# Low parts of 64 weight blocks made on VectorE instead of GpSimd, in a two-layer encoder trunk

## The chip, the cores and the metric

The kernel runs on 1 core of one Trainium2 chip. The metric is device time in microseconds, the median of several executions; one more execution is taken with the hardware profiler. The core's engines are named as the profile names them: PE (TensorE, matmuls; PEld its weight loads), DVE (VectorE), ACT (ScalarE), POOL (GpSimd) and SP (SyncE, which starts the transfers).

## The reference, cut to what matters

One step of a streaming encoder with two layers, for a prompt of 1024 rows and a sample of 64 rows that share all weights. All in float32.

```python
for i in range(2):
    hn = rmsnorm(x, norm_mix_g[i])
    x = x + (pool_mix(hn, ...) if i == 0 else hgrn_mix(hn, ...))
    x = x + conv_ffn(rmsnorm(x, norm_ffn_g[i]), ...)
x = rmsnorm(x, norm_out_g)

def pool_mix(h, ...):             # four windows, 256 columns each
    d = windowed_mean(h) - h      # causal, windows of 2, 4, 8, 16 rows
    return concat([d[g] @ w[g] for g in range(4)]) * scale

def conv_ffn(h, hist, w_up, cw, cb, w_down):
    gate, val = split(h @ w_up)   # 1024 -> 2 x 2816
    conv = cb + sum(cw[j] * shifted(gate, j) for j in range(3))
    return (silu(conv) * val) @ w_down
```

Layer 1's mixer is HGRN2, a gated linear recurrence in chunks of 64 rows.

## The kernel before, in words

**Layout.** The rows (1024 of the prompt, 64 of the sample) lie along the free axis in three chunks, 384, 384 and 256 + 64 columns; the model's 1024 features lie on 128 partitions x 8. `x` stays in SBUF for the whole run.

**Products in three terms.** A float32 product is made of fp32r products. Every weight block of 128 x 512 arrives raw (f32) in one of five buffers of the pool `raw`, by a transfer that SP starts (L134). ACT casts it to its high part `whi` (L128) and POOL subtracts to get the low part `wlo` = raw - whi (L129). With the activations split in the same way (`split`, L185 and L186: `hnhi` and `hnlo`, `hh` and `hl`), `mm3` issues three matmuls for each product: whi by the high part (L180), whi by the low part (L181), wlo by the high part (L182).

**The weight queue.** `load_ready` (line 109) goes through `queue` in order. A block is taken when one of 8 slots (a pair of `whi` and `wlo`) is free, and `drop` frees a slot when PE's last use of it has been issued. The raw buffer is free again for SP's next load when the subtract that reads it is done. The keys are ("pw", g, half) for the pooling mixer's pointwise weights, ("up", layer, block, part) and ("dn", layer, block, half) for the ConvFFN, and others for the HGRN mixer. For some parts `q_mix` loads two raw blocks and adds or subtracts them on DVE first (L152).

**Layer 0's mixer.** `token_sums` and `pool_diffs` scale the window matrices by each row's 1/rms (`rstd`, a Newton chain of small DVE steps, L333 to L344; `wr`, L544) and multiply (`pd`, L565); `pool_mix` multiplies by `pw` into `pe` and DVE updates `x` (L594).

**Norms.** `norm` sums the squares of `x` over the 8 feature blocks (L366, L373 into `acc_f`), PE transposes the sum (`nps_f`, L378), `rstd` gives the factor, and DVE makes the normed rows (L417).

**ConvFFN.** The 22 blocks of 128 hidden features are taken two at a time, 11 groups. Group 0 (blocks 0 and 1) makes plain products with the parts a11, a12, a21 and a22. From group 1 (blocks 2 and 3) on, chunks 0 and 1 are multiplied together as a 2 x 2 block product with seven products, whose mixed activations `sums` makes on DVE (sums at L437 and L449, split at L186) while group 0 and the start of group 1 run, and whose mixed weights come from `q_mix` (nine parts). Products land in banks `px`, `py`, `pz`; DVE adds them up in `e` (L713); ACT copies the gate (`ge`, L684); the convolution is two steps on DVE (L630, L631) between two on ACT; `hidden` multiplies and splits (L640, L642); `down` multiplies by the `dn` weights into `dn` banks, and DVE adds each to `x` (L757), which frees the bank (five banks, pool `pB`).

**Who sets the order.** PE's order is a schedule written by hand: tasks are generators whose yields carry costs, and `run` merges them under `tc.manual_schedule`. DVE, ACT, POOL and SP are ordered by the Tile scheduler, so an instruction that changes its engine shifts its neighbours on both. Each engine issues in order and waits in order.

Of the kernel before, what the change touches and what calls it, by code (L numbers as in the profile page):

```python
# [9 lines left out]
F32 = mybir.dt.float32  # L10
# [4 lines left out]
ALU = mybir.AluOpType  # L15
# [50 lines left out]
def trunk_kernel(ctx: ExitStack, tc: tile.TileContext, xtok, xs_tok, hist_tok, xf, par, gmix, pw, winm, ident_in,  # L66
                 masks_in, w_up, w_dn, w_in, w_out, s0, y_out, npool, nhg, nconv):
    nc = tc.nc
# [37 lines left out]
    free = [(i, False) for i in range(NR)]  # L106
    extra_w = []

    def load_ready(most=None):

        while queue and (most is None or len(loaded) < most):
            ph, key, make = queue[0]
            own = [p for p in free if p[1]] if ph == "g" and key[:2] not in (("out", H - 2), ("out", H - 1)) else []
            p = own[0] if own else next((p for p in free if not p[1]), None)
            if p is None:
                return
            free.remove(p)
            queue.pop(0)
            places[key] = p
            i, extra = p  # L120
            nm = "_".join(str(k) for k in key)
            if extra:
                hi, lo = (extra_w[i // 2][:, (i % 2 * 2 + b) * HW_:(i % 2 * 2 + b + 1) * HW_] for b in range(2))
            else:
                hi = wp.tile([P, HW_], F32R, name=f"whi{nm}", tag=f"whi{i}", bufs=1)
                lo = wp.tile([P, HW_], F32R, name=f"wlo{nm}", tag=f"wlo{i}", bufs=1)
            src = make(nm)
            nc.scalar.copy(hi, src)  # L128
            nc.gpsimd.tensor_tensor(lo, src, hi.bitcast(F32), op=ALU.subtract)  # L129
            loaded[key] = (hi, lo)  # L130

    def raw_block(nm, src, i):
# [24 lines left out]
    def drop(*keys):  # L157

        for k in keys:
            p = places.pop(k)  # L160
            free.append(p)
        load_ready()
# [320 lines left out]
    def token_sums(c):  # L483
# [19 lines left out]
        if c == 0:  # L503
            for i in (1, 0):
                nc.sync.dma_start(wm[i], winm[i])
            nc.sync.dma_start(ident, ident_in)
            load_ready(2)
            nc.sync.dma_start(prm, par)
# [13 lines left out]
        if c == 0:  # L522
            load_ready(6)
# [656 lines left out]
```

## Time and profile before

| | us |
|---|---|
| median of 3 executions (2372.25 to 2373.45) | 2372.37 |
| the profiled execution | 2377.06 |
| its span in the profile | 2375.2 |
| PE busy | 2284.7 (96%) |
| DVE busy | 1613.8 (68%) |
| POOL busy | 1003.0 (42%) |
| ACT busy | 904.3 (38%) |

The mean granted clock of PE is 0.981 of full speed. The span is that of the profiled execution and is 1.9 us shorter than its time; it is cut into stretches below. Busy time of an engine is the time in which it runs instructions of its own, not the time in which it waits. Idle time is put down to the instruction that ended it (the releaser). Where consecutive instructions of one kind are shown in one row, "x2" or "x3" stands at its end and the duration is that of all.

### The profile page before, as it was taken

How to read it: one execution, taken by the hardware profiler on the slowest of the kernel's cores; microseconds unless marked ns; L12 is line 12 of the kernel's file. 1: busy time of each engine (PE TensorE's matmuls, PEld its weight loads, DVE VectorE, ACT ScalarE, POOL GpSimd, SP SyncE). 2: the span in 40 equal slices, each digit the busy share in tenths (PEclk: the TensorE clock that was granted, in tenths of full speed). 3: DMA queues.
4: the chain of work that ended last, by engine and by line, in shares of the span. 5: the costliest groups of instructions: out<-in, count | busy, mean ns of one | idle time of the engine just before them, and what ended most of it. 6: DMA issues, size and time to landing. Idle time of an engine off the chain costs nothing. (4 is left out here: it accounts for less than half of the span.)

```text
span 2375.2 us, 38111 instructions
## 1 busy us (share of the span) xinstructions
PE 2284.7 (96%) x13830; PEld 2231.3 (94%) x13830; DVE 1613.8 (68%) x3728; ACT 904.3 (38%) x1965; POOL 1003.0 (42%) x1054
## 2 busy tenths in 40 slices
PE   9889999999999989999999999889999999999996
PEld 8889999999999989999999999878999999999996
DVE  6786656566666688767667767778766666666567
ACT  5444333334433353323323322345333333443335
POOL 1155554556655562112112211224454555564555
PEclk8999999999999999999999999989999999999998
DMA  7123333333433321001011000102343334433431
GB/s 233 49 81 116 125 121 120 123 125 129 138 116 125 124 69 36 26 18 54 26 35 40 32 26 22 36 25 76 111 130 116 125 119 134 134 124 117 129 120 76
DMA packets 118099, 218.70 MB, mean 92 GB/s; under 512 B 13436, under 2 KB 17404, under 8 KB 117528
## 3 DMA queue, kind: packets, MB, share of 16 engines
q1 hardware_dynamic: 117822, 216.15, 28.0%
q8 instruction: 109, 1.79, 0.3%
q14 instruction: 78, 0.64, 0.1%
q10 hardware_dynamic: 90, 0.12, 0.0%
HBM read 210.51 MB, written 5.72 MB: 91 GB/s over the span
## 5 line engine op out<-in xcount | busy, mean ns | idle before, releaser
L129 POOL TENSOR_TENSOR wloup_a<-rawup_a,whiup_a 128x512 fp32r<-128x512 f32 x368 | 513.1, 1411 | 568.1 <-ACT whiup_a L128 534.4
L128 ACT CAST whiup_a<-rawup_a 128x512 fp32r<-128x512 f32 x368 | 224.2, 617 | 573.8 <-PE dn L181 397.4
L152 DVE TENSOR_TENSOR rawup_a<-rawup_a,rawup_a 128x512 f32<-128x512 f32 x200 | 186.6, 933 | 286.4 <-DMA rawup_a<-w_up_in 261.4
L180 PE MATMUL dn<-hh,whidn 128*128 128x384 f32 (+1 forms) x1056 | 351.5, 333 | 11.5 <-DVE x L757 8.0
L181 PE MATMUL dn<-hl,whidn 128*128 128x384 f32 (+1 forms) x1056 | 348.7, 330 | 0.7 <-DVE hl L186 0.7
L182 PE MATMUL dn<-hh,wlodn 128*128 128x384 f32 (+1 forms) x1056 | 348.9, 330 | 0.0
L757 DVE TENSOR_TENSOR x<-x,dn 128x384 f32<-128x384 f32 (+1 forms) x528 | 262.3, 528 | 97.1 <-PE dn L182 95.5
L180 PEld LDWEIGHTS dn<-hh,whidn 128*128 128x128 f32 x1056 | 200.2, 190 | 18.0 <-DVE x L757 13.4
L181 PEld LDWEIGHTS dn<-hl,whidn 128*128 128x128 f32 x1056 | 200.1, 190 | 1.3 <-DVE hl L186 1.3
L182 PEld LDWEIGHTS dn<-hh,wlodn 128*128 128x128 f32 x1056 | 200.1, 189 | 0.0
L180 PE MATMUL pj<-hnhi,whiin 128*128 128x384 f32 (+1 forms) x528 | 185.0, 350 | 1.1 <-ACT hnhi L185 1.1
L181 PE MATMUL pj<-hnlo,whiin 128*128 128x384 f32 (+1 forms) x528 | 173.0, 328 | 2.4 <-POOL hnlo L186 2.4
L182 PE MATMUL pj<-hnhi,wloin 128*128 128x384 f32 (+1 forms) x528 | 173.2, 328 | 0.0
L630 DVE SCALAR_TENSOR_TENSOR cv<-ge,prm,cv 128x322 f32<-128x322 f32 (+1 forms) x132 | 132.1, 1002 | 48.2 <-ACT cv L629 42.0
L129 POOL TENSOR_TENSOR wlodn<-rawdn,whidn 128x512 fp32r<-128x512 f32 x88 | 119.0, 1354 | 100.9 <-ACT whidn L128 76.8
L960 DVE COPY_PREDICATED at<-masks,pl 128x64 f32<-128x64 uint8 (+7 forms) x432 | 117.0, 293 | 50.5 <-PE pl L945 48.8
L632 ACT ACTIVATE cv<-cv 128x322 f32<-128x322 f32 (+1 forms) x132 | 67.2, 509 | 161.3 <-DVE cv L631 160.9
L180 PE MATMUL pv<-hnhi,whiup_a 128*128 128x320 f32 (+1 forms) x384 | 122.1, 318 | 0.0
L180 PE MATMUL pg<-hnhi,whiup_a 128*128 128x320 f32 (+1 forms) x384 | 122.1, 318 | 0.0
L182 PE MATMUL pg<-hnhi,wloup_a 128*128 128x320 f32 (+1 forms) x384 | 121.7, 317 | 0.0
L182 PE MATMUL pv<-hnhi,wloup_a 128*128 128x320 f32 (+1 forms) x384 | 121.5, 317 | 0.0
L181 PE MATMUL pg<-hnlo,whiup_a 128*128 128x320 f32 (+1 forms) x384 | 121.5, 316 | 0.0
(1234 smaller groups left out, 6199.0 us busy)
## 6 DMA issues: line engine op xcount, KB each, us to landing
rawup_a<-w_up_in SPq DMA_DIRECT2D x568, 256.0 KB, 2.8
rawdn<-w_dn_in SPq DMA_DIRECT2D x88, 256.0 KB, 3.1
rawin<-w_in_in SPq DMA_DIRECT2D x64, 256.0 KB, 2.6
rawupp_a<-w_up_in SPq DMA_DIRECT2D x16, 256.0 KB, 2.7
rawout<-w_out_in SPq DMA_DIRECT2D x16, 256.0 KB, 2.7
xt<-xtok_in SPq DMA_DIRECT2D x7, 448.0 KB, 6.7
x<-xf_in SPq DMA_DIRECT2D x2, 1536.0 KB, 8.7
y_out<-x SPq DMA_DIRECT2D x8, 384.0 KB, 2.3
```

The lines of the kernel that those rows point to most:

```text
L128: nc.scalar.copy(hi, src)
L129: nc.gpsimd.tensor_tensor(lo, src, hi.bitcast(F32), op=ALU.subtract)
L152: nc.vector.tensor_tensor(t[0], t[0], t[1], op=bs[2])
L180: nc.tensor.matmul(ps, w[0][:, wsl], a_hi, start=first, stop=False, skip_group_check=more)
L181: nc.tensor.matmul(ps, w[0][:, wsl], a_lo, start=False, stop=False, skip_group_check=more)
L182: nc.tensor.matmul(ps, w[1][:, wsl], a_hi, start=False, stop=last, skip_group_check=more)
L630: nc.vector.scalar_tensor_tensor(t[:, :wd], ge[:, 0:wd], prm[:, cw[0]:cw[0] + 1], t[:, :wd], op0=ALU.mult, op1=ALU.add)
L632: nc.scalar.activation(t[:, :wd], t[:, :wd], AF.Silu)
L757: nc.vector.tensor_tensor(x[c][:, d, :], x[c][:, d, :], pd[:, :n], op=ALU.add)
L960: nc.vector.copy_predicated(dst[:, :, :, d * hh:], mk, a)
```

## The change

A function chooses the engine for the low part by the block's key: DVE for all of the pooling mixer's pointwise weights, for the up weights of ConvFFN blocks 0 to 3 and the down weights of blocks 0 and 1, in both layers; POOL for the rest. Of the subtracts at L129 (now L132), 64 move: 4 of `pw`, and per layer 26 of `up` (4 plain parts for each of two blocks, 9 parts for each of the next two) and 4 of `dn`. The instruction is otherwise the same. Behind the three added lines every line number of the kernel is 3 higher.

```diff
     extra_w = []
+
+    def lo_engine(ph, key):
+        return nc.vector if key[0] == "pw" or key[0] in ("up", "dn") and key[2] < (4, 2)[key[0] == "dn"] else nc.gpsimd
 
     def load_ready(most=None):
...
             src = make(nm)
             nc.scalar.copy(hi, src)
-            nc.gpsimd.tensor_tensor(lo, src, hi.bitcast(F32), op=ALU.subtract)
+            lo_engine(ph, key).tensor_tensor(lo, src, hi.bitcast(F32), op=ALU.subtract)
             loaded[key] = (hi, lo)
```

What it does to DVE's order is shown at three places. The first is DVE at the start of layer 0's mixer: `nt_p` is the Newton chain, `wr` the scaled window matrices that `pd` reads. Before:

```order
L343 TENSOR_TENSOR nt_p_202<-nt_p_202 128x4
L344 SCALAR_TENSOR_TENSOR nt_p_202<-nt_p_202 128x4
L544 TENSOR_SCALAR wr_214<-wm_105,nt_p_202 96x384
L544 TENSOR_SCALAR wr_218<-wm_104,nt_p_202 112x384
L463 TENSOR_TENSOR lbt<-prm 128x8
```

With the change:

```order
L347 SCALAR_TENSOR_TENSOR nt_p_202<-nt_p_202 128x4
L547 TENSOR_SCALAR wr_214<-wm_105,nt_p_202 96x384
L132 TENSOR_TENSOR wlopw_0_150<-rawpw_0_151,whipw_0_149 128x512
L547 TENSOR_SCALAR wr_218<-wm_104,nt_p_202 112x384
L132 TENSOR_TENSOR wlopw_1_156<-rawpw_1_157,whipw_1_155 128x512
```

Two low parts of the pointwise weights now stand behind the first and behind the second `wr`.

The second place is DVE in the third norm ahead of layer 0's ConvFFN (chunk 2): `acc_f` are the sums of squares, the last row ends them. Before:

```order
L366 TENSOR_TENSOR acc_f_1018<-acc_f_1018,sq_f_1022 128x320
L366 TENSOR_TENSOR acc_f_1019<-acc_f_1019,sq_f_1025 128x320
L152 TENSOR_TENSOR rawup_2_a_0_1405<-rawup_2_a_0_1405,rawup_2_a_3_1407 128x512
L366 TENSOR_TENSOR acc_f_1018<-acc_f_1018,sq_f_1028 128x320
L366 TENSOR_TENSOR acc_f_1019<-acc_f_1019,sq_f_1031 128x320
L630 SCALAR_TENSOR_TENSOR cv_1_0_1068<-ge_1_0_1064,prm,cv_1_0_1068 128x384
L366 TENSOR_TENSOR acc_f_1018<-acc_f_1018,sq_f_1034 128x320
L366 TENSOR_TENSOR acc_f_1019<-acc_f_1019,sq_f_1037 128x320
L631 SCALAR_TENSOR_TENSOR cv_1_0_1068<-ge_1_0_1064,prm,cv_1_0_1068 128x384
L373 TENSOR_TENSOR acc_f_1019<-acc_f_1019,acc_f_1018 128x320
```

With the change:

```order
L132 TENSOR_TENSOR wloup_1_a_995<-rawup_1_a_0_996,whiup_1_a_994 128x512
L132 TENSOR_TENSOR wloup_1_a_1001<-rawup_1_a_1_1002,whiup_1_a_1000 128x512
L132 TENSOR_TENSOR wloup_1_a_1007<-rawup_1_a_2_1008,whiup_1_a_1006 128x512
L132 TENSOR_TENSOR wloup_1_a_1013<-rawup_1_a_3_1014,whiup_1_a_1012 128x512
L369 TENSOR_TENSOR acc_f_1018<-acc_f_1018,sq_f_1022 128x320
L369 TENSOR_TENSOR acc_f_1019<-acc_f_1019,sq_f_1025 128x320
L369 TENSOR_TENSOR acc_f_1018<-acc_f_1018,sq_f_1028 128x320
L369 TENSOR_TENSOR acc_f_1019<-acc_f_1019,sq_f_1031 128x320
L369 TENSOR_TENSOR acc_f_1018<-acc_f_1018,sq_f_1034 128x320
L369 TENSOR_TENSOR acc_f_1019<-acc_f_1019,sq_f_1037 128x320
L155 TENSOR_TENSOR rawup_2_a_0_1405<-rawup_2_a_0_1405,rawup_2_a_3_1407 128x512
L376 TENSOR_TENSOR acc_f_1019<-acc_f_1019,acc_f_1018 128x320
```

Four low parts of block 1's up weights now stand ahead of the sums, and the two convolution steps of group 0 have gone behind them.

The third place is DVE in group 1 of layer 0, ahead of the addition to `e` of block 2 (`sum` and `mix0w` are the mixed activations, `cv` the convolution). Before:

```order
L449 TENSOR_TENSOR sum_1477<-row0w_930,row0q_873 128x384
L449 TENSOR_TENSOR sum_1479<-row0w_930,row0x 128x384
L449 TENSOR_TENSOR sum_1481<-row0w_930,row0q_873 128x384
L630 SCALAR_TENSOR_TENSOR cv_1_2_1505<-ge_1_2_1498,prm,cv_1_2_1505 128x322
L152 TENSOR_TENSOR rawup_2_a_2_1650<-rawup_2_a_2_1650,rawup_2_a_3_1652 128x512
L631 SCALAR_TENSOR_TENSOR cv_1_2_1505<-ge_1_2_1498,prm,cv_1_2_1505 128x322
L186 TENSOR_TENSOR mix0w_1568<-sum_1475,mix0w_1568 128x384
L186 TENSOR_TENSOR mix0w_1568<-sum_1477,mix0w_1568 128x384
L713 TENSOR_TENSOR e_2_1566<-e_2_1566,px_2_1573 128x384
```

With the change:

```order
L452 TENSOR_TENSOR sum_1477<-row0w_930,row0q_873 128x384
L452 TENSOR_TENSOR sum_1479<-row0w_930,row0x 128x384
L452 TENSOR_TENSOR sum_1481<-row0w_930,row0q_873 128x384
L132 TENSOR_TENSOR wloup_2_a_1493<-rawup_2_a_2_1494,whiup_2_a_1492 128x512
L633 SCALAR_TENSOR_TENSOR cv_1_2_1505<-ge_1_2_1498,prm,cv_1_2_1505 128x322
L132 TENSOR_TENSOR wlodn_0_0_1523<-rawdn_0_0_1524,whidn_0_0_1522 128x512
L634 SCALAR_TENSOR_TENSOR cv_1_2_1505<-ge_1_2_1498,prm,cv_1_2_1505 128x322
L132 TENSOR_TENSOR wlodn_1_0_1541<-rawdn_1_0_1542,whidn_1_0_1540 128x512
L189 TENSOR_TENSOR mix0w_1568<-sum_1475,mix0w_1568 128x384
L189 TENSOR_TENSOR mix0w_1568<-sum_1477,mix0w_1568 128x384
L716 TENSOR_TENSOR e_2_1566<-e_2_1566,px_2_1573 128x384
```

One low part of an up weight and two of the down weights have come in ahead of the addition; the raw sum of L152 has left this piece.

## Rows read from the trace of the kernel before

**Rows 1.** The page, part 1: busy time, share of the span and instructions
```profile
PE 2284.7 (96%) x13830; PEld 2231.3 (94%) x13830; DVE 1613.8 (68%) x3728; ACT 904.3 (38%) x1965; POOL 1003.0 (42%) x1054
```

**Rows 2.** Stretches: length, busy per engine, clock, DMA share, GB/s
```profile
120.00:180.00 60.00, 53.61 (x326) 51.87 (x325) 53.92 (x92) 27.75 (x59) 34.45 (x30) 1.00 0.26 84
300.00:360.00 60.00, 60.00 (x368) 60.00 (x367) 35.15 (x59) 22.77 (x44) 34.91 (x39) 1.00 0.39 128
1580.00:1640.00 60.00, 53.52 (x313) 51.03 (x311) 54.27 (x105) 33.60 (x71) 23.29 (x27) 0.97 0.17 54
```

**Rows 3.** Waits of PE, 120 to 180: us in total, times, longest
```profile
PE px L181 <- DVE hnlo L186: 1.9, 1, 1.9
PE py L180 <- ACT ge L684: 1.9, 1, 1.9
PE px L180 <- DVE e L713: 1.6, 1, 1.6
PE dn L180 <- DVE x L757: 0.9, 1, 0.9
```

**Rows 4.** Waits of PE, 1620 to 1680
```profile
PE px L180 <- ACT hnhi L185: 2.8, 2, 2.6
PE px L181 <- DVE hnlo L186: 2.3, 2, 1.9
PE dn L180 <- DVE x L757: 1.6, 2, 1.1
```

**Rows 5.** Waits of PE in 0 to 60, 60 to 120, 1500 to 1560
```profile
PE pd L565 <- DVE wr L544: 3.9, 1, 3.9
...
PE nps_f L378 <- DVE acc_f L373: 6.1, 2, 3.9
...
PE pl L945 <- DVE q__16127 L936: 7.3, 2, 3.9
```

**Rows 6.** Timeline of DVE, 136 to 162: start, us, line, operation
```profile
137.21 1.20 DVE L437 TENSOR_TENSOR sum<-row0w,row0x 128x384 f32<-128x384 f32 x1
...
140.84 1.65 DVE L437 TENSOR_TENSOR sum<-row0w 128x384 f32<-128x384 f32 x1
...
144.44 0.55 DVE L437 TENSOR_TENSOR sum<-row0q,row0w 128x384 f32<-128x384 f32 x1
...
153.00 1.54 DVE L186 TENSOR_TENSOR hl<-hr,hh 128x320 fp32r<-128x320 f32 x1
...
160.67 0.48 DVE L186 TENSOR_TENSOR hl<-hr,hh 128x320 fp32r<-128x320 f32 x1
```

**Rows 7.** POOL: two pieces of its timeline; its group on the page
```profile
12.47 1.26 POOL L129 TENSOR_TENSOR wlopw<-rawpw,whipw 128x512 fp32r<-128x512 f32 x1 [11.54 <-ACT whipw L128]
...
140.45 3.19 POOL L129 TENSOR_TENSOR wloup_a<-rawup_a,whiup_a 128x512 fp32r<-128x512 f32 x2
...
L129 POOL TENSOR_TENSOR wloup_a<-rawup_a,whiup_a 128x512 fp32r<-128x512 f32 x368 | 513.1, 1411 | 568.1 <-ACT whiup_a L128 534.4
```

**Rows 8.** Timeline of DVE, 1619 to 1642, first and last of the hits
```profile
1620.22 2.59 DVE L437 TENSOR_TENSOR sum<-row1w 128x384 f32<-128x384 f32 x3
...
1640.85 1.62 DVE L186 TENSOR_TENSOR hnlo<-sum,hnhi 128x384 fp32r<-128x384 f32 x1
```

**Rows 9.** DVE's sum of two raw blocks: one of the timeline; the group
```profile
156.80 0.68 DVE L152 TENSOR_TENSOR rawup_a<-rawup_a,rawup_a 128x512 f32<-128x512 f32 x1
...
L152 DVE TENSOR_TENSOR rawup_a<-rawup_a,rawup_a 128x512 f32<-128x512 f32 x200 | 186.6, 933 | 286.4 <-DMA rawup_a<-w_up_in 261.4
```

**Rows 10.** Timeline of DVE: Newton steps near 12, 46 and 1527
```profile
12.34 0.16 DVE L338 TENSOR_TENSOR nt_p<-nt_p 128x4 f32<-128x4 f32 x1
12.54 1.22 DVE L339 SCALAR_TENSOR_TENSOR nt_p<-nt_p 128x4 f32<-128x4 f32 x1
...
46.51 1.20 DVE L342 TENSOR_SCALAR nt_f<-nt_f 128x3 f32<-128x3 f32 x1
...
1527.21 1.23 DVE L340 TENSOR_TENSOR nt_g<-nt_g 128x3 f32<-128x3 f32 x1
```

## The prediction

> **What bounds the kernel now.** I read the busy shares first. TensorE (PE) is busy for 96% of the span; VectorE (DVE) for 68%, GpSimd (POOL) for 42% [rows 1]. The table of stretches says where the missing 4% lies: in the middle of a ConvFFN PE has 60.00 of 60 us and DVE 35, so nothing given to DVE there can be seen; in the 60 us in which each ConvFFN opens, PE loses about 6.5 us and DVE is busy for 54 of 60 [rows 2]. So the change is judged by PE's own waits, and by DVE in the openings. The waits of PE in the two openings [rows 3, 4] and in three other stretches [rows 5] name a DVE instruction as the releaser nearly everywhere, and ACT where it runs behind DVE. None names POOL's low part: PE never waits for the thing whose engine is changed.
>
> What it waits for is DVE's list, and that list is slowed. A subtract or sum of DVE of 128x384 takes 0.55 us when alone and 1.65 when a low part of POOL runs beside it: the call at 140.84 lies on POOL's pair of 140.45 [rows 6, 7]. Calls that read one input from PSUM keep their time in the same stretch. From the first to the last I count eight long calls ahead of the e<-px that PE waits for at 158.8 us: 1.20 at 137.21, 1.64, 1.65, 1.65, a pair of 2.86 (1.02 when not hit), 1.65, and 1.54 against 0.48 at 153.00 [rows 6]. Their excess is 0.65 + 1.09 + 1.10 + 1.10 + 1.84 + 1.10 + 1.06 = 7.9 us. In layer 1 the same count from the triple at 1620.22 (2.59 against 1.49) to the 1.62 at 1640.85 gives eight hits and 8.2 us [rows 8]. POOL's subtracts are lengthened too: 1.26 alone, 1.41 in the mean, 3.19 for a pair [rows 7].
>
> **The change part by part.** 64 subtracts go from POOL to DVE: the mixer's 4, and in each layer 26 of up weights and 4 of down weights. PE's order is the same. Nothing is removed, and no DMA is added; a raw buffer is now given back to SP's next weight load by a DVE instruction.
>
> *Price of one on DVE.* No DVE subtract with an fp32r result of this size is in the trace. The nearest row is the sum of two raw blocks, same shape, both inputs in SBUF: 0.68 us unhit, 0.93 in the mean with its hits [rows 9]. I take 0.68, because the subtract that hit it is the one that moves; 0.93 stays as the upper bound. A lower bound is 0.55 x 512/384 = 0.73 less the 0.1 by which neighbours overlap: 0.6.
>
> *Layer 0, first two groups.* Ahead of e<-px the changed DVE order holds eight moved subtracts, and one raw sum (L152) has gone behind it. Gain 7.9 + 0.68 - 8 x 0.68 = 3.2 us earlier, out of the 1.9 + 1.9 + 1.6 that PE waits there [rows 3]. The wait of 0.9 for the x update of the down product goes too, since DVE is then ahead. Term: **4.1**.
>
> *Layer 1, first two groups.* 8.2 - 8 x 0.68 - 0.47 (a sum of L449 that now comes earlier) = 2.3; I take 2.0 of the 5.1 of px, as part of it waits for ACT [rows 4]. The two dn waits of 1.6 go. Term: **3.6**.
>
> *Start.* One Newton step is hit: 1.22 instead of 0.16, with POOL's wlopw running [rows 7, 10]. Without it wr comes 1.06 earlier, the second wr only 0.4, since wlopw now stands between them. The products pd wait for the first [rows 5]. Term: **0.6**. First norm: two steps are hit, the second taking 1.20 [rows 10], which gives back 2.0; two moved calls cost 1.36; of the 0.64 PE sees about **0.5**.
>
> *Third norm of layer 0.* Here the change costs. Four moved subtracts (2.7 us) come ahead of the sums of squares, on whose end (acc_f) PE waits up to 3.9 us [rows 5]; in exchange the two conv steps and the raw sum between them move behind or later, 0.61 + 0.61 + 0.68 back. Term: **-0.8**.
>
> *End of the HGRN mixer.* The steps of the Newton chain at 1524 to 1531 are hit several times (1.23 against 0.16) [rows 10], partly by POOL's sums of squares, which stay. Two hits go (2.0), two moved calls come (1.4): **0.6**, against waits of 7.3 us at pl [rows 5].
>
> Everything else lies in stretches where PE is full, and DVE has 25 us of 60 free: nothing. What would take that cover away is a DVE instruction that waits in order for an ACT cast whose slot PE has not freed; behind it stand the x updates that free the five PSUM banks of dn. A slot is freed ahead of those updates, so I price this at nothing and give it a rival. For SP: the raw buffer that DVE returns comes about 2 us later than from POOL, and the load then still reaches its slot before PE's use of it.
>
> Sum: 4.1 + 3.6 + 0.6 + 0.5 - 0.8 + 0.6 = 8.6. The profiled execution took 2377.1 us (its span 2375.2 and 1.9 around it), 4.7 above the median of the runs: 2368.5 for a like profile, and 2372.4 - 8.6 = **2363.8 us** for the runs. With 0.93 for each of the sixteen priced calls the openings lose 4.0 and the sum is 4.6 (2367.8); with 0.6 they gain 1.3 (2362.5).
>
> A rule that speaks against this: the Trainium skill, Perfetto Trace Analysis, section Identifying the Most-Contended Engine, has the engine of highest occupancy relieved first; of the two at hand that is DVE (68% against 42%), and the change loads it by 44 us. By it the kernel would lose; the trace shows why the share misleads here: DVE is idle where PE is full, and in the openings its time goes to hits.
>
> **The rivals.** (a) *Given back.* The relief comes, but the next waiter on PE is late as well, such as ACT's casts, or a DVE wait in order for a raw block. For it: the py wait names ACT [rows 3], the longest px wait of layer 1 does too [rows 4]. Against: ACT's input there comes from DVE. Then only the start and a third of the openings stay: 2.6 + 0.5, less 0.8, some 2 us: 2370.
>
> (b) *Slower: the hits do not go, DVE only gets longer.* If the long calls come from the order in which DVE and POOL happen to start, or from something else in the openings, the moved calls are pure load: eight at 0.6 in each opening (4.8 + 4.8), four each at the third norm and at the start (2.4 + 1.8, less what PE has free), 0.6 and 1.2 at the HGRN end and the first norm, together 15.6: 2388. It decides from the point where a moved call costs more than the relief per call, 7.9 / 8 = 0.99 us; the row nearest is 0.68. For it: some hits in the HGRN stretch are from POOL work that stays. Against: all sixteen hits of the openings lie on a low part. The Trainium skill, SBUF — State Buffer, section Who interferes with whom, says that a DVE instruction with two SBUF inputs contends with a POOL instruction that reads SBUF, and that the order of issue decides who blocks. The trace agrees on the first: 1.65 against 0.55; by the second POOL alone would be held where DVE starts first, and the rows show both lengthened.
>
> (c) *More.* DVE being ahead removes the whole of the openings' waits (6.3 + 6.7), and the start, the first norm and the HGRN end give their full hits (1.1 + 2.0 + 1.4): 17.5 us, 2355. For it: once DVE keeps up, the queue no longer grows. Against: eight new calls stand in each opening.
>
> **How the numbers follow.** A difference of about 0.2% (4.7 us) is what a measurement of this kernel can tell from no change: faster is below 2367.6, slower above 2377.1. Chances: forecast 0.48 (2360 to 2368), more (c) 0.16, given back (a) 0.21, slower (b) and its milder forms 0.15. Faster 0.64, same 0.21, slower 0.15. The range takes in the forecast, most of (c) and all of (a) but not (b): **2356 to 2376**; the likeliest case alone is 2360 to 2368.
>
> **What would show it.** Right: in the changed profile DVE's sums and subtracts at 137 to 155 and 1620 to 1641 us are at 0.55, the new DVE subtracts at 0.6 to 0.7, PE's waits for px, py and dn in the openings fall from 13 to about 5 us, pd starts near 14.2 instead of 15.24, and the wait for acc_f in the third norm grows. Given back: the same DVE rows, but PE's waits keep their sum under another name. Wrong: DVE rows stay at 1.65, or the new subtracts take 1.0 or more; or a wait appears in the full stretches, at dn or at a weight load, where rows 2 show none.

## The result and the profile after

| | us |
|---|---|
| kernel before, median of 6 (2371.96 to 2375.55) | 2372.85 |
| changed kernel, median of 6 (2352.36 to 2364.69) | 2363.62 |
| ratio | 0.995, 95% interval 0.9933 to 0.9967 |
| profiled execution, before and after | 2377.06 and 2364.69 |
| the changed kernel twice more, each beside the kernel before | 0.9964 (0.9951 to 0.9977) and 0.9928 (0.9911 to 0.9946) |

The forecast was 2363.8 us; the gain is 9.2 us in the medians and 12.4 between the two profiled executions. Three sets of runs put it between 8 and 16 us.

Part 1 of the page of the changed kernel:

```profile
PE 2281.5 (97%) x13830; PEld 2229.7 (94%) x13830; DVE 1609.8 (68%) x3792; ACT 905.4 (38%) x1965; POOL 915.6 (39%) x990
```

DVE has 64 instructions more than in [rows 1], and is busy for 4.0 us less (0.3 and 8.0 less in the two later profiles of the changed kernel). POOL is busy for 87 us less: 64 subtracts of 1.3 to 1.4 us. The price of a moved one is in the view of its source line: instructions on DVE, shortest / median / longest in ns, first and last start.

```profile
L132 DVE TENSOR_TENSOR wloup_a<-rawup_a,whiup_a x52: 676/685/784, 28.6 to 1686.2; 128x512 fp32r<-128x512 f32 x52
...
L132 DVE TENSOR_TENSOR wlodn<-rawdn,whidn x8: 678/683/693, 150.8 to 1640.7; 128x512 fp32r<-128x512 f32 x8
...
L132 DVE TENSOR_TENSOR wlopw<-rawpw,whipw x4: 681/682/682, 13.8 to 28.0; 128x512 fp32r<-128x512 f32 x4
```

The price is 0.68 us, the row of L152 that was taken for it [rows 9]; 64 of them are 43.8 us, and the hits (DVE calls lengthened beside a subtract on POOL) that went gave back at least as much. In DVE's timeline of the changed kernel, the calls of the opening (line numbers 3 higher than in [rows 6]):

```profile
135.37 0.55 DVE L440 TENSOR_TENSOR sum<-row0w,row0x 128x384 f32<-128x384 f32 x1
...
138.31 0.55 DVE L440 TENSOR_TENSOR sum<-row0w,row0f 128x384 f32<-128x384 f32 x1
...
144.55 1.02 DVE L189 TENSOR_TENSOR hnlo<-sum,hnhi 128x384 fp32r<-128x384 f32 x2
...
147.02 0.48 DVE L189 TENSOR_TENSOR hl<-hr,hh 128x320 fp32r<-128x320 f32 x1
...
153.44 0.54 DVE L716 TENSOR_TENSOR e<-e,px 128x384 f32<-128x384 f32 x1
```

The calls that took 1.20, 1.65 and 1.54 us take 0.55, 0.55 and 0.48, and the pair of 2.86 takes 1.02. The addition to `e` starts at 153.44 instead of the 158.81 of the kernel before:

```profile
158.81 0.54 DVE L713 TENSOR_TENSOR e<-e,px 128x384 f32<-128x384 f32 x1
```

Of these 5.4 us, 1.8 were won ahead of 136 us already (the `hr` of 136.74 starts at 134.91 now), and 3.5 in this piece. Layer 1's opening shows the same:

```profile
1613.27 1.02 DVE L440 TENSOR_TENSOR sum<-row1w 128x384 f32<-128x384 f32 x2
...
1620.23 0.55 DVE L440 TENSOR_TENSOR sum<-row1w,row1x 128x384 f32<-128x384 f32 x1
```

PE's waits in the changed kernel, the stretches 0 to 60, 60 to 120, 120 to 180, 1580 to 1620 and 1620 to 1680 one after the other, the main ones:

```profile
PE pd L568 <- DVE wr L547: 2.0, 2, 1.8
...
PE nps_f L381 <- DVE acc_f L376: 3.9, 2, 2.2
PE pg L185 <- DVE wloup_a L132: 3.4, 1, 3.4
...
PE px L183 <- DVE e L716: 2.7, 1, 2.7
...
PE pg L185 <- DVE wloup_a L132: 1.3, 1, 1.3
...
PE px L183 <- ACT hnhi L188: 1.4, 2, 1.0
PE px L184 <- DVE hnlo L189: 0.7, 2, 0.5
```

Against [rows 3] the four waits of layer 0's opening (6.3 us) are one of 2.7. Against [rows 4] the 6.7 us of layer 1 are 2.1 (the waits at pz are counted below). Against [rows 5] pd waits 2.0 instead of 3.9 and acc_f 3.9 instead of 6.1. Two waits are new: PE waits for the low part itself, 3.4 us in layer 0 and 1.3 in layer 1. In the stretches of [rows 2] PE is now at 57 and 56 of 60 us in the openings:

```profile
120.00:180.00 60.00, 57.34 (x357) 57.02 (x356) 55.66 (x113) 27.74 (x59) 14.12 (x14) 1.00 0.29 93
...
1580.00:1640.00 60.00, 56.34 (x319) 53.49 (x319) 51.31 (x113) 31.82 (x68) 10.26 (x17) 0.94 0.21 67
```

The mean granted clock over the span rose too, from 0.981 to 0.983: of the span, (1 - 0.981) x 2375.2 = 45 us were lost to the lower of PE's two levels before, and 0.017 x 2362.9 = 40 now. By the pages, PE's idle time (span less busy time) fell by 9.1 us, from 90.5 to 81.4, and its busy time, for the same 13830 matmuls, by 3.2. So of the 12.4 us between the profiled executions 3 to 5 come by the clock, and the waits bring the rest. (The clock has three digits, so each product is known to about 1 us; it is an upper bound, because part of the low stretches lies where PE waits anyway. The two levels are 1.2 and 2.4 GHz.) The spread of the three sets is the clock's as well. Span times granted clock, an estimate of the time at full clock, fell by 8.1 us in the first of the two repeats (in the mean of the runs, 2328.8 to 2320.7) and by 9.7 in the second (2333.3 to 2323.6); the loss to the lower level stayed at 45 us in the first repeat and fell by 6 in the second.

### The profile page after: what moved, and what is told of

Its sections match the earlier page's. It is cut to its first block, busy times and chain, and to the rows that moved or that the text cites. A ratio compares the mean times of both kernels' runs of the same rounds, so it can differ in the third digit from the quotient of the medians.

```text
span 2362.9 us, 38081 instructions
## 1 busy us (share of the span) xinstructions
PE 2281.5 (97%) x13830; PEld 2229.7 (94%) x13830; DVE 1609.8 (68%) x3792; ACT 905.4 (38%) x1965; POOL 915.6 (39%) x990
## 4 chain that ended last, share of the span: by engine, by line
PE 81%; DVE 11%; DMA 3%; ACT 2%; POOL 2%; issue 1%; SPq 0%; DVEq 0%; POOLq 0%; ACTq 0%
PE dn L183 6%; PE dn L185 6%; PE dn L184 6%; PE pj L183 5%; PE pj L184 5%; PE pj L185 5%; PE pz L184 3%; PE pz L183 3%; PE pz L185 3%; PE pl L948 3%; PE pg L183 2%; PE py L184 2%; PE py L185 2%; PE px L184 2%; PE py L183 2%; PE pg L185 2%
## 5 line engine op out<-in xcount | busy, mean ns | idle before, releaser
L132 POOL TENSOR_TENSOR wloup_a<-rawup_a,whiup_a 128x512 fp32r<-128x512 f32 x316 | 441.1, 1413 | 462.5 <-ACT whiup_a L131 432.0
L155 DVE TENSOR_TENSOR rawup_a<-rawup_a,rawup_a 128x512 f32<-128x512 f32 x200 | 180.7, 904 | 275.4 <-DMA rawup_a<-w_up_in 251.2
L633 DVE SCALAR_TENSOR_TENSOR cv<-ge,prm,cv 128x322 f32<-128x322 f32 (+1 forms) x132 | 127.2, 965 | 45.0 <-ACT cv L632 41.5
L132 POOL TENSOR_TENSOR wlodn<-rawdn,whidn 128x512 fp32r<-128x512 f32 x80 | 106.2, 1328 | 88.2 <-ACT whidn L131 73.9
```

The lines of the kernel that those rows point to most:

```text
L132: lo_engine(ph, key).tensor_tensor(lo, src, hi.bitcast(F32), op=ALU.subtract)
L155: nc.vector.tensor_tensor(t[0], t[0], t[1], op=bs[2])
L633: nc.vector.scalar_tensor_tensor(t[:, :wd], ge[:, 0:wd], prm[:, cw[0]:cw[0] + 1], t[:, :wd], op0=ALU.mult, op1=ALU.add)
```

## The experiments

The theory: a POOL subtract that reads SBUF holds up a DVE call with two inputs in SBUF by 1.1 us; in the openings DVE's list sets when PE goes on. The rivals: the gain comes from DVE's new order or the raw buffers; any POOL work beside DVE does it; DVE's length does not decide. Each of the three sets below had its own runs of the kernel before (medians 2375.0, 2375.8 and 2379.0), so a run is compared by its ratio to those, or with a run of its own set. The edits are shown against the changed kernel. Only one profile of the kernel before is there, that of the result above, and traces are compared with it.

### The low parts on neither engine

```diff
-            lo_engine(ph, key).tensor_tensor(lo, src, hi.bitcast(F32), op=ALU.subtract)
+            if lo_engine(ph, key) is nc.vector:
+                lo = hi
+            else:
+                nc.gpsimd.tensor_tensor(lo, src, hi.bitcast(F32), op=ALU.subtract)
```

> The 64 low parts that the change moves are not made at all (their third product uses the high part again), so neither POOL nor DVE has them. Theory (POOL's subtracts lengthen DVE's calls, and DVE's list sets PE's waits in the openings): the relief comes without its price on DVE. The waits that the changed kernel still has there go as well (3.4 and 1.3 us of pg for a low part, 2.7 and 2.1 of px): 12 to 20 us faster than the kernel before, 2353 to 2361, and DVE's sums of 128x384 at 0.55 us in the openings. Rival (the gain comes from somewhere else, such as another order of DVE's list or the raw buffers given back later): within 4 us of the kernel before, 2369 to 2376.

Measured: 2347.19 us, ratio 0.9881 (0.9863 to 0.99), 27.8 us faster than the kernel before. That is outside what was expected, on the far side. The stretches of the two openings:

```profile
1580.00:1640.00 60.00, 60.00 (x374) 59.68 (x372) 46.51 (x107) 29.84 (x64) 7.79 (x18) 1.00 0.27 88
1640.00:1700.00 60.00, 60.00 (x364) 59.88 (x364) 37.57 (x64) 27.23 (x54) 26.61 (x32) 1.00 0.39 132
120.00:180.00 60.00, 60.00 (x375) 60.00 (x374) 47.06 (x100) 26.90 (x57) 10.46 (x14) 1.00 0.29 97
```

PE has no wait left in either opening, and its clock is at full in all three stretches. The theory stands, and its scale was too small, mostly by what the clock gives: between the two profiled executions (2377.1 and 2343.8) PE's idle time fell by 21.1 us and its busy time by 12.1, with the mean granted clock at 0.985, 35 us lost instead of 45. By the ratios of the three sets the changed kernel is 11 to 20 us behind this one. That is what DVE's price, the two new waits and the clock behind them still cost; how it is shared among them is not shown.

### One more DVE instruction for each block, POOL as before

```diff
+            nc.gpsimd.tensor_tensor(lo, src, hi.bitcast(F32), op=ALU.subtract)
+            if lo_engine(ph, key) is nc.vector:
+                nc.vector.tensor_reduce(spare, hi.bitcast(F32), axis=AX.X, op=ALU.add)
...
```

> The kernel before, with one more DVE instruction for each of the 64 blocks: a reduction of the 512 columns of the high part into one spare column, while POOL makes the low part as before. Theory (DVE's list is what PE waits for in the openings): eight to nine calls of about 0.6 us in each opening, four more each in the third norm and at the start: 8 to 16 us slower, 2380 to 2388. Rival (DVE's length does not decide, only POOL's): within 4 us of the kernel before.

Measured: 2391.18 us, ratio 1.0062 (1.0041 to 1.0082), 16.2 us slower, just beyond the far end of what the theory expects. The reduction takes 0.67 us, nearly the price of the subtract:

```profile
L135 DVE TENSOR_REDUCE spare<-whiup_a x52: 667/674/687, 31.0 to 1713.3; 128x1 f32<-128x512 f32 x52
```

PE's waits in 120 to 180 and 1640 to 1700:

```profile
PE px L186 <- DVE e L719: 3.8, 1, 3.8
PE py L186 <- ACT ge L690: 3.1, 1, 3.1
PE px L186 <- DVE hr L648: 1.0, 1, 1.0
...
PE px L186 <- ACT hnhi L191: 6.2, 1, 6.2
```

With those at pz, PE's waits rose by 2.6 us in layer 0's opening and by 1.9 in layer 1's, and the longest at acc_f by 1.5 (5.5 instead of 3.9). So DVE's length counts in the openings, and the price on DVE is real: the change pays it, and gets back more. DVE's order alone does not make the gain either, as these calls stand in nearly the same places as the moved subtracts. This is also the rival of the prediction that ended slower, run by itself: the load without the relief costs 16 us, where 15.6 was worked out. But the agreement is luck: the rival counted waits, and between the profiled executions PE's idle time rose by only 5.7 us (90.5 to 96.2), its busy time by 9.4. The larger part is the clock: 0.976, 57 us lost instead of 45.

### POOL at work, but reading nothing

```diff
+            if lo_engine(ph, key) is nc.vector:
+                nc.gpsimd.memset(lo.bitcast(F32), 0.0)
...
```

> POOL writes zeros into the 64 low parts (a memset of the same 128x512 tile) in place of the subtraction, so POOL is still at work beside DVE but reads nothing from SBUF; the low products are left out by this. Theory (it is POOL's reading beside a DVE call with two inputs that holds DVE): DVE's sums are at 0.55 us, and the time is that of the run without low parts, 2353 to 2361. Rival (any POOL work beside DVE holds it): DVE's sums stay at 1.2 to 1.65 us and the time within 5 us of the kernel before, 2368 to 2377.

Measured: 2344.54 us, ratio 0.9873 (0.9853 to 0.9892), the time of the run without low parts and, like it, below the 2353 to 2361 that was expected. POOL's and DVE's timelines of this kernel at the same moment:

```profile
137.88 0.52 POOL L133 MEMSET wlodn<- 128x512 f32 x1
139.38 0.53 POOL L133 MEMSET wlodn<- 128x512 f32 x1 [0.97 <-PE pv L188]
```

```profile
137.83 0.55 DVE L443 TENSOR_TENSOR sum<-row0gt,row0f 128x384 f32<-128x384 f32 x1
138.30 0.55 DVE L455 TENSOR_TENSOR sum<-row0w 128x384 f32<-128x384 f32 x1
...
139.64 0.55 DVE L455 TENSOR_TENSOR sum<-row0w,row0q 128x384 f32<-128x384 f32 x1
```

DVE's sums with two inputs in SBUF run beside POOL's memsets in their full 0.55 us. The memset is shorter (0.53 against 1.28) and starts earlier, as it doesn't wait for the cast; but no sum in the openings is lengthened at all. So it is not any POOL work that holds DVE. The Trainium skill, SBUF — State Buffer, section Who interferes with whom, says that a DVE instruction with two SBUF inputs contends with a POOL instruction that reads SBUF and not with one that only writes it: the traces agree, 1.65 us beside a subtract before [rows 6] and 0.55 beside a memset here.

Both of the runs without subtractions also give the raw buffers back earlier, so they do not exclude that rival by themselves. The trace of before speaks against it: from 120 to 165 us DVE waits for no raw block (its only wait is one of 0.5 us for ACT), and PE's waits in the openings name no weight [rows 3, 4].

### The same subtractions in two halves on POOL

```diff
+            for o in range(0, HW_, HW_ // 2 if lo_engine(ph, key) is nc.vector else HW_):
...
+                nc.gpsimd.tensor_tensor(lo[:, s_], src[:, s_], hi.bitcast(F32)[:, s_], op=ALU.subtract)
```

> The kernel before, with each of the 64 subtractions made by POOL in two halves of 256 columns. If a DVE call is held for what is left of the POOL instruction under way: hits of 0.4 to 0.6 us instead of 1.1, with up to twice as many, time from 5 us faster to the same as before (2369 to 2376). If a hit has a fixed length: twice as many of 1.1 us, 8 to 16 us slower.

Measured: 2377.99 us, ratio 1.0002 (0.9991 to 1.0014): no difference. The timeline of DVE shows why:

```profile
142.10 1.09 DVE L191 TENSOR_TENSOR mix0vt<-sum,mix0gt 128x384 fp32r<-128x384 f32 x1
143.12 1.09 DVE L191 TENSOR_TENSOR mix0vt<-sum,mix0S 128x384 fp32r<-128x384 f32 x1
144.13 1.02 DVE L636 SCALAR_TENSOR_TENSOR cv<-ge,prm,cv 128x322 f32<-128x322 f32 x1
145.08 1.08 DVE L191 TENSOR_TENSOR hnlo<-sum,hnhi 128x384 fp32r<-128x384 f32 x1
```

A hit is now 1.09 - 0.55 = 0.54 us, half of the 1.10 beside a whole subtract, and there are more of them: from 135 to 154 us fourteen, with two smaller ones 7.7 us in all, where eight came to 7.9 before. A DVE call is held for about one POOL instruction, at both lengths tried; shorter pieces of the same work do not help here.

### The two halves of the change

```diff
-        return nc.vector if key[0] == "pw" or key[0] in ("up", "dn") and key[2] < (4, 2)[key[0] == "dn"] else nc.gpsimd
+        return nc.vector if key[0] == "up" and key[2] in (2, 3) or key[0] == "dn" and key[2] < 2 else nc.gpsimd
```

> Only the low parts of blocks 2 and 3's up weights and of blocks 0 and 1's down weights on DVE (44 of the 64); the pointwise weights and blocks 0 and 1's up weights on POOL as before. Theory (the gain is made where the mixed activations are summed and made on DVE): nearly all of the gain, 7 to 11 us faster than before; the waits of pg for a low part (3.4 and 1.3 us in the changed kernel) are gone and acc_f is waited for again (3.9). Rival (the start and the norms carry half of it): 3 to 5 us faster.

Measured, with the changed kernel beside it: 2366.68 us, ratio 0.9965 (0.9953 to 0.9977), 9.1 us faster, as the theory expects. The changed kernel in the same set:

> The changed kernel once more, beside its parts on one chip. 8 to 11 us faster than the kernel before on that chip (2361 to 2366).

It came to 2367.65, ratio 0.9964 (0.9951 to 0.9977), 8.1 us faster. So the 44 low parts of the openings carry as much as all 64. The other 20 alone:

```diff
...
+        return nc.vector if key[0] == "pw" or key[0] == "up" and key[2] < 2 else nc.gpsimd
```

> The other 20 alone: the pointwise weights and blocks 0 and 1's up weights on DVE. Theory: the start gains 1 to 2 us, the third norm loses about 1 (pg waits 3.4 for a low part, acc_f 2.2 less), layer 1's first group gains or loses about 1: within 3 us of the kernel before. Rival: 4 to 6 us faster.

Measured: 2374.28 us, ratio 0.9992 (0.9983 to 1.0001), 1.5 us in the medians, which can't be told from nothing. In its waits, 60 to 120, stands what the changed kernel has there:

```profile
PE nps_f L381 <- DVE acc_f L376: 3.4, 2, 2.2
PE pg L185 <- DVE wloup_a L132: 3.4, 1, 3.4
```

### Block 1's up weights back on POOL

Where the new wait of 3.4 us comes from, DVE's timeline of the changed kernel shows; four low parts in one row, behind the `x` updates of the mixer:

```profile
100.53 0.54 DVE L597 SCALAR_TENSOR_TENSOR x<-pe,prm,x 128x320 f32<-128x320 f32 x1
100.99 2.49 DVE L132 TENSOR_TENSOR wloup_a<-rawup_a,whiup_a 128x512 fp32r<-128x512 f32 x4
```

The kernel before made them on a POOL that was otherwise idle, each as soon as its cast was there:

```profile
94.32 1.32 POOL L129 TENSOR_TENSOR wloup_a<-rawup_a,whiup_a 128x512 fp32r<-128x512 f32 x1 [23.21 <-ACT whiup_a L128]
96.08 1.28 POOL L129 TENSOR_TENSOR wloup_a<-rawup_a,whiup_a 128x512 fp32r<-128x512 f32 x1 [0.44 <-ACT whiup_a L128]
```

```diff
-        return nc.vector if key[0] == "pw" or key[0] in ("up", "dn") and key[2] < (4, 2)[key[0] == "dn"] else nc.gpsimd
+        return nc.vector if key[0] == "pw" or key[0] == "up" and key[2] in (0, 2, 3) or key[0] == "dn" and key[2] < 2 else nc.gpsimd
```

> The changed kernel with block 1's up weights (four in each layer) back on POOL, which is idle where they are made. Theory (on DVE they stand behind the x updates of the mixer, so PE waits 3.4 us in layer 0 and 1.3 in layer 1 for a low part, and that wait is bought with 2.2 less at acc_f): 1 to 4 us faster than the changed kernel. Rival (the wait only changes its name, acc_f is late by as much): the same within 1 us.

Measured: 2361.73 us, ratio 0.9936 (0.9923 to 0.9948), 5.9 us below the changed kernel of the same set, more than the 1 to 4 expected. Because the runs of one kernel spread over some 10 us, it was run again beside the changed kernel:

> The changed kernel with block 1's up weights back on POOL, once more, beside the changed kernel on one chip. If the wait of pg for a low part is a true cost: 2 to 6 us faster than the changed kernel in the medians. If the difference seen before lies in the spread of the runs: the same within 1.5 us.

> The changed kernel, for comparison with the two others of this set: 8 to 11 us faster than the kernel before.

Measured: 2358.98 us, ratio 0.9909 (0.9895 to 0.9923), against 2363.03, ratio 0.9928 (0.9911 to 0.9946). The changed kernel is 15.9 us faster than the kernel before here, not the 8 to 11 expected. The second difference between the two versions is 4.0 us with intervals that overlap; in the first they are 0.0003 apart. Both have the same sign and size, so I take this version, at 14 to 20 us below the kernel before, as the fastest complete one here, with a lead over the change of 4 to 6 us in the medians. That the lead comes from the waits is not shown: span times clock differs by only 0.7 us in the first of the two sets (in the mean, 2320.7 and 2320.0) and by 0.8 in the other (2323.6 and 2322.8), so most of the lead is the clock. Its waits in 60 to 120 are those of the kernel before at acc_f, and none for a low part:

```profile
PE nps_f L381 <- DVE acc_f L376: 6.1, 2, 3.9
PE pe L183 <- DVE x L597: 1.4, 3, 0.8
```

The wait at acc_f grew by 2.2 us in exchange for the 3.4 and 1.3 of pg that went, and px in layer 1's opening is waited for 3.1 us instead of 2.1: 1.5 net. With block 0's up weights on POOL as well:

> The pointwise weights and group 1's weights on DVE, all of blocks 0 and 1's up weights on POOL. If block 0's four on DVE do nothing: the time of the kernel with block 1 alone on POOL, within 2 us. If they help the norm after the mixer's first chunk (two Newton steps are held up by 1.0 us each there when POOL makes them): 2 to 3 us slower than that.

Measured: 2365.7 us, ratio 0.9937 (0.9919 to 0.9956), 6.7 us above the kernel with only block 1 on POOL (2 to 3 were expected) and 2.7 above the changed one. DVE's two hits in the first norm are back (1.16 and 1.18 us), and PE waits for pl at the end of the HGRN mixer for 8.1 us, against 6.2 with block 0 on DVE. So the eight low parts of block 0 look worth having on DVE; the intervals still overlap (0.9919 against 0.9923) and span times clock is only 0.5 us apart, so the size stays uncertain.

## Why the prediction was right, point by point

**The bound.** Right. PE's waits in the openings were the main place to win; they fell from 6.3 and 6.7 us to 2.7 and 2.1.

**The price, 0.68.** Right to the digit for one call [rows 9]; 0.93 was too wide. But what counts in a list of calls is the time from start to start, and that is the prediction's lower bound: four in a row take 2.49 us (the row at 100.99 above), 0.60 from one to the next. With it the sum for layer 0's opening is 7.9 + 0.60 - 8 x 0.60 = 3.7 us, where 3.2 was forecast and DVE's list came out 3.5 shorter.

**Layer 0's opening, 4.1.** The px and py waits fell from 5.4 to 2.7, by 2.7 where 3.2 was worked out, and the dn wait of 0.9 went: 3.6 us, and 0.7 more at pz behind them (1.0 before, 0.3 now).

**Layer 1's opening, 3.6.** 6.7 - 2.1 = 4.6 us: the dn waits went, and px gained 3.0 where 2.0 was taken. Another 0.5 was gained at pz (1.0 before, 0.5 now).

**Start, 0.6.** About right. The first `wr` starts 1.35 us earlier (13.43 instead of 14.78): 1.04 for the Newton step that is no longer hit, and 0.31 because the rows landed earlier in this execution. From the 1.04 goes a new wait of 0.25 for the second `wr`: 0.8. PE's wait for pd fell by more, from 3.9 to 2.0, because its filling matmuls ahead of it ended 0.8 later (at 12.12 instead of 11.30):

```profile
13.90 0.69 PE L568 MATMUL pd<-wr,xt 96*128 96x96 f32 x4 [1.77 <-DVE wr L547]
14.83 3.50 PE L568 MATMUL pd<-wr,xt 112*128 112x96 f32 x20 [0.25 <-DVE wr L547]
```

**First norm, 0.5.** About right: pe's waits for DVE fell by 1.1 us, and 0.8 at an earlier acc_f are new.

**Third norm, -0.8.** The size held, the mechanism did not. The prediction said that PE never waits for a low part, and priced only the delay of acc_f. It named a longer wait for acc_f as a sign of being right. But acc_f is waited for 2.2 us less, and PE waits 3.4 for the low part: -1.2. The first follows from the second, since PE now comes later to acc_f; with block 1 back on POOL the 3.9 is there again. What was true of POOL, that it made the low parts in time, was carried over to DVE, where the same instruction stands at the end of a list. The order showed the four in a row ahead of the sums; that they stood behind `x` updates that follow PE was not asked.

**End of the HGRN mixer, 0.6.** pl waits 6.2 instead of 7.3, and another wait of 0.7 at pl is gone (it is there again in the profile of the changed kernel's second repeat); 1.3 came as the second wait for a low part: 0.5.

**The full stretches, nothing.** Nearly. Outside of the openings PE's waits at dn come to 6.0 us instead of 5.5. The one at 372.6 us is new, which the prediction named as a sign against itself; that rows 2 show no such wait holds for the one stretch that they show. The second wait below, at 1001.5 us in the HGRN mixer, is in two profiles of the changed kernel and not in that of its second repeat, so the runs do not show that the change makes it:

```profile
PE dn L183 <- DVE x L760: 0.7, 1, 0.7
...
PE pl L975 <- DVE k__10572 L939: 1.5, 1, 1.5
```

**The sum.** By PE's waits 4.3 + 5.1 + 1.9 + 0.3 - 1.2 + 0.5 - 0.5 - 1.5 = 8.9, near the 9.1 by which its idle time fell, where 8.6 was forecast; with the 3.2 of its busy time this makes up the 12.4 between the profiled executions. The clock was in no term. That the median lies within 0.2 us of the forecast is luck, in a kernel whose runs spread over 12 us and with single terms that were off by up to 1.5 each way; the sign and the size of the gain are not.

**Rivals.** Given back: a part of it happened, as the wait at `e` grew from 1.6 to 2.7. Slower: its condition failed, the hits went. More: not reached by the change, but by the run without low parts, at 2347, below the 2355 that was worked out: 21.1 us of idle time went instead of 17.5, and the rest is the clock.

## What to carry to other kernels

Moving work from POOL to a DVE that is nearly full can shorten DVE's list, where each POOL instruction that reads SBUF holds up a two-input DVE call by more than the work costs on DVE (1.1 against 0.60 to 0.68 us here); count the hits ahead of the wait that sets the end, stretch by stretch, not the busy shares. Ask of each moved instruction what stands ahead of it in its new queue: what was early on an idle engine is late on a busy one, and can become PE's own wait.

## What the runs showed of the hardware that was not expected

- A hit is nearly as long as the POOL instruction it meets: 1.10 us beside 512 columns (1.26 to 1.28 alone), 0.54 beside 256 (0.72 alone), and none beside a memset.
- Whether a DVE call has one input or two does not settle alone if it is hit. The 64 reductions, with one, took 0.667 to 0.687 us, the one at 147.00 too, which ran beside a pair of subtracts on POOL (145.04 to 148.23). But a Newton step with one input took 1.20 us at 46.51 [rows 10], beside a pair on POOL from 45.18 to 47.68, where the same step took 0.17 unhit.
- PE's granted clock can fall behind its waits and add to them. Three stretches, of the kernel before, of the run with one more DVE instruction, and (in the experiment above) of the run without low parts: in layer 1's opening, after waits of px of up to 2.6 us, the mean granted clock was 0.85 in the 20 us from 1640; after a wait of 6.2 us it was 0.89 over 60 us; with no wait it was 1.00 from 1580 to 1700. It does not fall behind every wait: with 6.3 us of waits in layer 0's opening it stayed at 1.00 [rows 2].

```profile
1640.00:1660.00 20.00, 18.15 (x101) 17.70 (x102) 15.37 (x22) 8.19 (x18) 12.15 (x14) 0.85 0.40 126
```

```profile
1640.00:1700.00 60.00, 50.24 (x264) 46.42 (x262) 49.83 (x88) 19.96 (x43) 23.91 (x24) 0.89 0.26 88
```

- From 1500 to 1700 us (the same work lies up to some 30 us earlier or later from run to run), the loss to the lower level ((1 - clock) x 200) was 18 us before and with one more DVE instruction, 12 to 16 in the three profiles of the change, and 8 without low parts and with the memset. So a wait that is taken away there may be worth more than its own length; how much of the loss follows from the waits was not tried by itself.
- Over whole spans the loss was 57 us with one more DVE instruction per block, 45 before, 40 with the change, 35 without low parts and 28 with the memset (0.012 x 2341.0). Not all of this is the waits: the same changed kernel lost 33 (0.014 x 2356.0) in its second repeat, since its first 60 us ran at 1.00 there and at 0.89 in the result's profile, as these two rows show; the memset run had 1.00 there too.

```profile
0.00:60.00 60.00, 54.47 (x348) 52.70 (x349) 40.08 (x111) 35.22 (x68) 0.41 (x8) 0.89 0.74 237
```

```profile
0.00:60.00 60.00, 54.37 (x383) 52.29 (x384) 46.13 (x124) 38.14 (x75) 0.41 (x8) 1.00 0.74 238
```
